# Trunk of attention and experts on one core: the residual sum in natural column order, normalised in place, a weight place freed for the stream, and the last expert columns in halves

## The chip, the core and the metric

The kernel runs on one core of a Trainium2 chip. The metric is device time in microseconds, the median of the runs shown; lower is better. Rows of the profile give times from the start of the span. TensorE (PE), VectorE (DVE), ScalarE (ACT), GpSimd (POOL) and SyncE (SP) are the engines; SyncE issues all DMAs here.

## What is computed

256 tokens of width 2048 pass through one layer: three attention branches, gates and an output projection w_o, a residual sum with a layer norm, then a mixture of 32 experts (each token goes to two experts of one group of eight), and a second residual sum with a layer norm:

```python
merged = g_a * (o_a @ w_up_a[l]) + g_b * (o_b @ w_up_b[l]) + g_c * (o_c @ w_up_c[l])
x = layer_norm(ALPHA * x + merged @ w_o[l], ln1_g[l], ln1_b[l])
y = hier_moe(x, w_grp[l], b_grp[l], w_rt[l], b_rt[l], w1[l], w3[l], w2[l])
x = layer_norm(ALPHA * x + y, ln2_g[l], ln2_b[l])
...
for e in range(N_EXPERTS):
    hid = jax.nn.silu(xt @ w1[e]) * (xt @ w3[e])
    out = out + comb[:, e:e + 1] * (hid @ w2[e])
```

All is float32. The experts' weights w1, w3 and w2 are 3 x 32 matrices of 4 MB, read once, 403 MB of the 540 MB that the kernel reads.

## The kernel before, in words

**Up to w_o.** Every projection is cut into units (`proj`, L175): `ld` loads 256 KB of weights into one of six places of a ring in the tile `stt` (L164, L186), `sp` splits it into a high and a low part (a cast on ScalarE, L155, a subtraction on VectorE, L156), `run` makes the matmuls (L215 to L217 for w_o). `emit` (L609) writes them out so that loads run five units and splits two units ahead of the matmuls. A ring place is loaded again when the split of its last load is done; SyncE issues in order, so a load that waits holds back all that stand behind it. Within these limits a scheduler orders an engine's instructions; those in `V(...)` keep the order of the program among themselves.

**w_o (L508 to L511).** 64 units: two halves of the contraction, each over column blocks `WO` (L437) of 512, 512, 512, 256 and 256. After the first half of a block `residual_sum` (L468) adds ALPHA * x, which `load_x` (L439) has put into the tile `wx` after unit `XL` (L44), and after the second half it adds the rest; the two token chunks of 128 are c = 0 and 1. `wx` holds the sum as [t, j, p], with the column blocks of the contraction contiguous, so that `row_stats` (L475), the transposes of `logit_step` (L501) and its logit matmuls (L505) read contiguous columns. Between the units, after those of `WOL` (L43), one part of the experts' stream is issued (`main.load`, L819).

**The stream (`Stream`, L665).** The experts' weights are parts of 2 MB, in the order of use, each loaded by SyncE into a free place of 16 KB a partition. The first parts go in halves of 1 MB (`HALVES`, L40). Places: four (`wk`, `wkk`), four (`wg`), `acc` and `yb` once each, and `wx`, once both token chunks are normalised out of it (L926). A place is loaded again when `used` (L740) tells that its part, or half of it, is through. The parts 0 to 8 are loaded up to the end of w_o; part 9 goes into `yb` (L887), part 10 into `wx` (L927), parts 11 to 14 into the places of parts 0 to 3, in halves.

**Between w_o and the experts (L885 to L927).** Per token chunk: statistics, 1/sqrt on GpSimd, then `normalise` (L830) writes the normalised sum in another layout into memory of `stt` and a tile `x1n`, four pieces of 512 columns, half of them on ScalarE, half on GpSimd; `route_steps` (L845) finds group, experts and positions on VectorE with a few small matmuls (L875), and a selection matrix S (L881). `keep_warm` (L629) puts small bf16 matmuls into TensorE's gaps, `KW` of them (6 and 6). Then `gather` (L988) picks the rows of each expert by matmuls with S (weights are the normalised sum, 128 x 128, L991), and `hidden` (L1025) makes the products, four experts beside each other. The first call of it does four of eight steps and frees the first halves of its places (L1067).

**The experts.** 8 rounds of four experts: h1 and h3, their product, transposes (L1096, of every second column), w2 (L1113), `combine` (L1035). The first norm's residual is added in rounds 1 to 4 (`residual`, L966).

**The end.** In the last round w2 comes in slices of 1024, 512 and 512 columns (`LAST`, L663; L725), one DMA for each expert of the four in a 512-column slice. `last_slices` (L1122) makes the products in four steps (k, j), `combine` copies 512 columns, multiplies them by the weights of the routing for both token chunks and adds; `chain` (L1190) makes a chunk's statistics, and `fast_tail` (L1175) the second norm and the stores.

## Time and profile before

| | us |
|---|---|
| median of 3 runs | 1681.29 (1680.66 to 1682.52) |
| profiled execution, its own time | 1680.39 |
| its span, first to last instruction | 1678.6 |
| TensorE busy | 1458.4 (87%) |
| VectorE busy | 615.0 (37%) |
| ScalarE busy | 456.0 (27%) |
| GpSimd busy | 12.6 (1%) |
| mean DMA rate over the span | 324 GB/s |

The profiled execution is 1.79 us longer than its span. Busy shares are means over stages of different kinds; a stage is to be read by its own rows. A matmul of two float32 operands shows as two records, a transpose as one.

### The profile page before, as it was taken

What the parts mean: (1) busy time and instruction counts of PE and PEld (TensorE: products, weight loads), DVE (VectorE), ACT (ScalarE), POOL (GpSimd) and SP (SyncE); (2) the same over time, 40 slices, a digit from 0 to 9 for tenths busy, and PEclk for the clock granted to TensorE, in tenths of its full rate; (3) what the DMA queues carried; (4) which work ended last, traced back from release to release, by engine and by line L of the source; (5) the groups of instructions that cost most, each with busy time, mean ns of one, the idle gap of its engine ahead of it and who ended that gap; (6) DMA issues with size and microseconds to landing.
All of it is one profiled execution on the core that took longest, in us unless ns stands there. A gap on an engine that the chain in (4) does not pass through costs nothing.

```text
span 1678.6 us, 20715 instructions
## 1 busy us (share of the span) xinstructions
PE 1458.4 (87%) x7984; PEld 878.5 (52%) x7984; DVE 615.0 (37%) x1165; ACT 456.0 (27%) x841; POOL 12.6 (1%) x24
## 2 busy tenths in 40 slices
PE   9999999999999999998976967967868768769758
PEld 8989988888878887883321322312312212213212
DVE  6656866566565676551120210200200101101005
ACT  5545455665545444441100000000000000000100
POOL 0000000000000000010000000000000000000000
PEclk9999999999999999999987987978978879879879
DMA  7766565555887558959999999999999999999996
GB/s 238 230 188 169 157 171 163 175 170 177 279 299 230 185 183 276 329 187 380 429 426 429 428 427 429 428 426 428 427 428 428 428 428 428 427 429 428 428 413 230
DMA packets 120203, 543.67 MB, mean 324 GB/s; under 512 B 13904, under 2 KB 28064, under 8 KB 94880
## 3 DMA queue, kind: packets, MB, share of 16 engines
q1 hardware_dynamic: 120096, 542.27, 84.5%
q8 instruction: 64, 1.05, 0.3%
q14 instruction: 43, 0.35, 0.1%
HBM read 540.10 MB, written 2.12 MB: 323 GB/s over the span
## 4 chain that ended last, share of the span: by engine, by line
PE 54%; DMA 42%; DVE 1%; issue 1%; ACT 1%; SPq 1%; POOL 0%; ACTq 0%; DVEq 0%; POOLq 0%
DMA wg<-in_w_dram 15%; DMA wk<-in_w_dram 15%; PE ps L216 10%; PE ps L217 9%; PE ps L215 9%; PE h L1030 9%; DMA wkk<-in_w_dram 5%; DMA wx<-in_w_dram 4%; PE yp L1113 3%; PE ps L210 3%; PE ps L207 3%; PE ps L209 3%; DMA stt<-in_w_gate_dram 1%; PE yp L1136 1%; DMA stt<-in_w_o_dram 1%
## 5 line engine op out<-in xcount | busy, mean ns | idle before, releaser
L156 DVE TENSOR_TENSOR wl<-stt,wh 128x512 fp32r<-128x512 f32 (+1 forms) x492 | 333.7, 684 | 238.7 <-ACT wh L155 237.4
L155 ACT CAST wh<-stt 128x512 fp32r<-128x512 f32 (+1 forms) x492 | 302.1, 616 | 315.0 <-PE ps L217 129.8
L1030 PE MATMUL h<-wg,xg 128*32 128x512 f32 x896 | 230.2, 703 | 74.3 <-DMA wg<-in_w_dram 74.2
L1030 PE MATMUL h<-wk,xg 128*32 128x512 f32 x704 | 200.8, 709 | 58.0 <-DMA wk<-in_w_dram 58.0
L215 PE MATMUL ps<-wh,xH 128*128 128x512 f32 (+2 forms) x512 | 198.1, 389 | 0.3 <-ACT wh L155 0.2
L216 PE MATMUL ps<-wl,xH 128*128 128x512 f32 (+2 forms) x512 | 195.3, 381 | 2.9 <-DVE wl L156 2.8
L217 PE MATMUL ps<-wh,xL 128*128 128x512 f32 (+2 forms) x512 | 194.8, 381 | 0.0
L1001 DVE TENSOR_SCALAR xg<-gp,g1n,b1n 128x128 f32<-128x128 f32 x56 | 22.9, 410 | 424.9 <-PE h L1030 373.6
L1030 PEld LDWEIGHTS h<-wg,xg 128*32 128x32 f32 x896 | 50.7, 126 | 190.0 <-DMA wg<-in_w_dram 101.9
L1030 PE MATMUL h<-wkk,xg 128*32 128x512 f32 x208 | 117.0, 718 | 18.2 <-DMA wkk<-in_w_dram 18.2
L1030 PE MATMUL h<-wx,xg 128*32 128x512 f32 x208 | 114.2, 703 | 12.1 <-DMA wx<-in_w_dram 12.1
L998 ACT ACTIVATE xg<-gp,b1n,g1n 128x128 f32<-128x128 f32 x56 | 25.6, 457 | 356.5 <-PE h L1030 252.5
L1030 PEld LDWEIGHTS h<-wk,xg 128*32 128x32 f32 x704 | 44.0, 127 | 144.1 <-DMA wk<-in_w_dram 81.2
L216 PEld LDWEIGHTS ps<-wl,xH 128*128 128x128 f32 x512 | 96.7, 189 | 22.6 <-DVE wl L156 5.4
L215 PEld LDWEIGHTS ps<-wh,xH 128*128 128x128 f32 x512 | 96.3, 189 | 18.3 <-ACT wh L155 1.6
L217 PEld LDWEIGHTS ps<-wh,xL 128*128 128x128 f32 x512 | 96.6, 189 | 17.4
L1113 PE MATMUL yp<-wg,yb 128*32 128x512 f32 x368 | 95.0, 595 | 6.8 <-DMA wg<-in_w_dram 6.8
L1113 PE MATMUL yp<-wk,yb 128*32 128x512 f32 x304 | 91.4, 596 | 7.0 <-DMA wk<-in_w_dram 7.0
L1039 DVE COPY yb<-yp 128x512 f32<-128x512 f32 x15 | 10.4, 691 | 189.9 <-PE yp L1113 173.0
L207 PE MATMUL ps<-xH,wh 128*128 128x256 f32 x256 | 73.3, 286 | 0.0
L210 PE MATMUL ps<-xH,wl 128*128 128x256 f32 x256 | 72.7, 284 | 0.2 <-DVE wl L156 0.2
L209 PE MATMUL ps<-xL,wh 128*128 128x256 f32 x256 | 72.6, 284 | 0.0
(322 smaller groups left out, 1991.9 us busy)
## 6 DMA issues: line engine op xcount, KB each, us to landing
wg<-in_w_dram SPq DMA_DIRECT2D x75, 2048.0 KB, 27.6
wk<-in_w_dram SPq DMA_DIRECT2D x57, 2048.0 KB, 28.2
stt<-in_w_gate_dram SPq DMA_DIRECT2D x192, 256.0 KB, 3.1
wx<-in_w_dram SPq DMA_DIRECT2D x20, 2048.0 KB, 27.1
wkk<-in_w_dram SPq DMA_DIRECT2D x18, 2048.0 KB, 30.2
stt<-in_w_in_dram SPq DMA_DIRECT2D x104, 256.0 KB, 3.0
stt<-in_w_o_dram SPq DMA_DIRECT2D x64, 256.0 KB, 5.8
wg<-in_w_dram SPq DMA_DIRECT2D x14, 1024.0 KB, 8.5
```

The source lines that it names most:

```text
L155: nc.scalar.copy(h, src)
L156: nc.vector.tensor_tensor(l, src, h.bitcast(F32), ALU.subtract)
L207: nc.tensor.matmul(o, hb, a.H(kt), start=st_ and b % 2 == 0, stop=False, skip_group_check=True)
L209: nc.tensor.matmul(o, hb, a.L(kt), start=False, stop=False, skip_group_check=True)
L210: nc.tensor.matmul(o, lb, a.H(kt), start=False, stop=sp_, skip_group_check=True)
L215: nc.tensor.matmul(o, ha, wh, start=st_, stop=False)
L216: nc.tensor.matmul(o, ha, wl, start=False, stop=False)
L217: nc.tensor.matmul(o, la, wh, start=False, stop=sp_)
L998: nc.scalar.activation(xg[:, kt], gp[:, j], AF.Identity, scale=g1n[:, kt:kt + 1], bias=b1n[:, kt:kt + 1])
L1001: nc.vector.tensor_scalar(xg[:, kt], gp[:, j], g1n[:, kt:kt + 1], b1n[:, kt:kt + 1], ALU.mult, ALU.add)
L1030: nc.tensor.matmul(h[32 * e:32 * e + 32, :], xg[:, 8 * c + j, 32 * e:32 * e + 32], wt[e][:, j, :], start=(c == 0 and j == 0), stop=(c == 1 ...
L1113: nc.tensor.matmul(yps[n][32 * e:32 * e + 32, :], hT[:, 2 * k + j, 32 * e:32 * e + 32], wt[e][:, j, n * 512:(n + 1) * 512], start=(k + j = ...
```

## The change

The sum is kept in natural column order: `x1p` is [t, 2048]; x is loaded into places of the staging ring, at later units (`XL`), and read from there with a stride; the transposes take every nj-th column (4th or 2nd). `normalise` works in place, on ScalarE alone, by 512 columns, and `gather` reads every 8th column. The tiles `stt` and the split weights' buffers are closed after w_o and their memory becomes `wq`, a place of the stream, loaded right behind `yb`; `wx` is no place any more. `keep_warm` is called six times, with one tile. Parts 11 to 14 go in a quarter, a quarter and a half, and the first product frees its places by quarters after two steps. In the last round a slice of 512 columns comes in two DMAs, one for the even and one for the odd rows of all four experts; the last step of the last slice and `combine_last` work in halves of 256 columns, the copy on ScalarE and VectorE; statistics of the second norm are over 256 columns.

```diff
-XL = (1, 5, 12, 18, 22)
-KW = (6, 6)
+XL = (3, 11, 19, 23, 27)
+KW = (6, 6, 6, 10, 4, 12)
...
-    wb = ctx.enter_context(tc.tile_pool(name="wb", bufs=1))
-    stt = wb.tile([P, 6 * 512], F32, name="stt")
...
-    wsp = ph1.enter_context(tc.tile_pool(name="wsp", bufs=3, side="right"))
+    wss = ExitStack()
+    wb = wss.enter_context(tc.tile_pool(name="wb", bufs=1, side="right"))
+    stt = wb.tile([P, 6 * 512], F32, name="stt")
+    wsp = wss.enter_context(tc.tile_pool(name="wsp", bufs=3, side="right"))
...
-            nc.sync.dma_start(x1p[c][:, kt:kt + w // P], xp[c * P:(c + 1) * P, kt:kt + w // P, :])
+            XR[i, c] = st = stg()[:, :w].rearrange("t (j p) -> t j p", p=P)
+            nc.sync.dma_start(st, xp[c * P:(c + 1) * P, kt:kt + w // P, :])
+    def cols_of(i, c):
+        o, w, _ = WO[i]
+        return x1p[c][:, o:o + w]
...
-        a = x1p[c][:, kt:kt + nj]
-        return nc.vector.scalar_tensor_tensor(a, a, 1.0 if half else ALPHA,
-                                              ps[:, :w].rearrange("t (p j) -> t j p", j=nj), ALU.mult, ALU.add)
-    def row_stats(c, k):
-        return nc.vector.bn_stats(R["st"][:, c, k // 2, :], x1p[c][:, k:k + 2].rearrange("t j p -> t (j p)"))
+        a = cols_of(i, c)
+        if half:
+            return nc.vector.scalar_tensor_tensor(a, a, 1.0, ps[:, :w], ALU.mult, ALU.add)
+        return nc.vector.scalar_tensor_tensor(a.rearrange("t (p j) -> t p j", j=nj),
+                                              XR.pop((i, c)).rearrange("t j p -> t p j"), ALPHA,
+                                              ps[:, :w].rearrange("t (p j) -> t p j", j=nj), ALU.mult, ALU.add)
+    def row_stats(i, c, k):
...
-            nc.tensor.transpose(tp[:, j, :], x1p[c][:, kt + j, :], ident)
+            nc.tensor.transpose(tp[:, j, :], cols_of(i, c)[:, j::nj], ident)
         xt = R["xs"] if nj == 4 else R["xs"][:, 2 * c:2 * c + 2]
-        R["xc"] = nc.scalar.copy(xt[:, :nj], tp[:, :nj])
+        V(nc.scalar.copy(xt[:, :nj], tp[:, :nj]))
+        if between:
+            between()
...
-                self.jobs = [(k, h) for k in u[:a] for h in range(2)] + [(k, None) for k in u[a:b]]
-                self.jobs += [(k, h) for h in range(2) for k in u[b:c]] + [(k, None) for k in u[c:]]
+                self.jobs = [(k, h) for k in u[:a] for h in ((0, 2), (2, 4))] + [(k, (0, 4)) for k in u[a:b]]
+                self.jobs += [(k, h) for h in ((0, 1), (1, 2), (2, 4)) for k in u[b:c]] + [(k, (0, 4)) for k in u[c:]]
...
+                if ne == 4:
+                    for j in range(2):
+                        nc.sync.dma_start(t.rearrange("p (x j n) -> p x j n", j=2, n=w)[:, :, j],
+                                          w2[4 * q:4 * q + 4, c * 256:(c + 1) * 256,
+                                             o:o + w].rearrange("x (p j) n -> p x j n", j=2)[:, :, j])
+                    return
...
+    wss.close()
+    wqp = ctx.enter_context(tc.tile_pool(name="wqp", bufs=1, reuse_waits="tile"))
+    wq = wqp.tile([P, W2D], F32, name="wq")
     main.add([yb2], True)
+    main.add([wq])
...
+    def normalise(c, *ks):
+        for k in ks:
+            v = x1p[c][:, 512 * k:512 * k + 512]
+            V(nc.scalar.activation(v, v, AF.Identity, scale=rs1[:, c:c + 1], bias=nb1[:, c:c + 1]))
...
+        normalise(c, *(range(4) if c else range(2)))
...
+    main.load()
...
-    keep_warm(KW[0])
-    logit_step(len(WO) - 1, 1)
+    warm = keep_warm(KW[0])
+    logit_step(len(WO) - 1, 1, lambda: keep_warm(KW[1], warm))
+    normalise(0, 2, 3)
+    keep_warm(KW[2], warm)
     for k in "ababab":
...
-    keep_warm(KW[1])
+    keep_warm(KW[3], warm)
     for k in "caca":
         next(steps[k])
-    main.add([wx])
-    main.load()
 
...
-                pin(nc.tensor.matmul(gp[:, j, :], x1n[c][k4 // 2][:, 4 * (k4 % 2) + j, :], S[:, c].rearrange("p e s -> p (e s)"),
+                pin(nc.tensor.matmul(gp[:, j, :], x1p[c][:, k4 // 2 * 1024 + k4 % 2 * 4 + j:(k4 // 2 + 1) * 1024:8], S[:, c].rearrange("p e s -> p (e s)"),
...
+            keep_warm(KW[4], warm)
             for _ in steps["c"]:
                 pass
+            keep_warm(KW[5], warm)
...
-                hidden(0, 0, "1", xg, h1, 0, 4)
+                hidden(0, 0, "1", xg, h1, 0, 2)
+                hidden(0, 0, "1", xg, h1, 2, 4)
...
+        def combine_last(o, yp, then=None):
+            cut = [slice(256 * h, 256 * h + 256) for h in range(2)]
+            y = yb[:, o:o + 512]
+            V2(nc.scalar.copy(y[:, cut[0]], yp[:, cut[0]]))
+            V2(nc.vector.tensor_copy(y[:, cut[1]], yp[:, cut[1]]))
+            for c in range(2):
+                cp = PS["pm"].tile([P, 512], F32, name=f"cp{q}{o}{c}", tag="lg" if c else "lt")
+                for h in cut:
+                    nc.tensor.matmul(cp[:, h], ScT[:, c, :], y[:, h], start=True, stop=True, skip_group_check=True)
+                for k, h in enumerate(cut):
+                    a = acc[c][:, o:o + 512][:, h]
+                    V2(nc.vector.tensor_tensor(a, a, cp[:, h], ALU.add))
+                    if then:
+                        then(c, k)
...
+                        cut = (0, 256, 512) if end and k + j == 2 else (0, 512)
...
+                            for a, b in zip(cut, cut[1:]):
+                                for e in range(4):
+                                    nc.tensor.matmul(yp[32 * e:32 * e + 32, a:b], hT[:, 2 * k + j, 32 * e:32 * e + 32],
+                                                     wt["n", q, k, (n, e // ne)][:, e % ne, j, i * 512 + a:i * 512 + b],
+                                                     start=(k + j == 0), stop=(k + j == 2), skip_group_check=True)
                 for i, yp in enumerate(yps):
```

## Rows read from the trace of the kernel before

**Rows 1.** The page's slices: the span in 40 equal parts of 42 us; the granted TensorE clock in tenths of full speed, and what the DMA moved.
```profile
PEclk9999999999999999999987987978978879879879
GB/s 238 230 188 169 157 171 163 175 170 177 279 299 230 185 183 276 329 187 380 429 426 429 428 427 429 428 426 428 427 428 428 428 428 428 427 429 428 428 413 230
```

**Rows 2.** Busy time by stretches: from:to in us, its length, then busy us (records) of PE, of PE's weight loads, DVE, ACT and POOL, the granted clock (1.00 is 2.4 GHz), the DMA share and GB/s.
```profile
660.00:670.00 10.00, 9.76 (x42) 7.55 (x41) 6.33 (x10) 5.31 (x9) 0.00 (x0) 1.00 1.04 403
735.00:747.00 12.00, 11.89 (x99) 11.29 (x98) 5.19 (x15) 4.20 (x8) 1.16 (x2) 1.00 0.01 2
760.00:762.20 2.20, 2.20 (x25) 0.47 (x17) 0.05 (x1) 0.46 (x1) 0.00 (x0) 1.00 0.02 7
764.50:1603.00 838.50, 647.24 (x3490) 211.83 (x3486) 106.46 (x182) 48.20 (x97) 0.00 (x0) 0.87 1.01 428
1632.00:1655.00 23.00, 19.24 (x106) 5.44 (x110) 5.76 (x10) 0.59 (x1) 0.00 (x0) 0.85 1.02 364
```

**Rows 3.** Timeline of SyncE around the end of w_o: start, us, the DMA issues of the stream's parts by the place that they fill.
```profile
746.97 0.34 SPq L733 DMA_DIRECT2D yb<-in_w_dram  x1
752.60 0.34 SPq L733 DMA_DIRECT2D wx<-in_w_dram  x1
762.24 1.28 SPq L733 DMA_DIRECT2D wk<-in_w_dram  x3
766.90 1.28 SPq L733 DMA_DIRECT2D wk<-in_w_dram  x3
```

**Rows 4.** w_o's loads. First the line of its DMA issues from 630 to 746 us, from issue to landing; then the waits of ScalarE in w_o (us in total, times, longest); then four rows of the timeline: two casts one unit apart, and the two places at 660 us where TensorE waits for late weights.
```profile
DMA to landing us min/median/max: 2.9/5.5/8.3
...
ACT wh L155 <- DMA stt<-in_w_o_dram: 15.4, 9, 2.8
...
725.68 0.62 ACT L155 CAST wh<-stt 128x512 fp32r<-128x512 f32 x1 [0.74 <-DVE wl L156]
...
727.04 0.62 ACT L155 CAST wh<-stt 128x512 fp32r<-128x512 f32 x1 [0.74 <-DVE wl L156]
...
660.60 0.19 PEld L215 LDWEIGHTS ps<-wh,mH 128*128 128x128 f32 x1 [0.45 <-ACT wh L155]
...
661.33 0.50 PE L216 MATMUL ps<-wl,mH 128*128 128x512 f32 x1 [0.22 <-DVE wl L156]
```

**Rows 5.** Transposes on TensorE. The weight loads of the two lines, with ns min/median/max, first and last start, and one burst of each from the timeline: L501 reads contiguous columns, L1096 every second one.
```profile
L501 PEld LDWEIGHTS xt<-ident,wx x32: 138/140/144, 704.4 to 747.7; 128*128 128x128 f32 x32
...
L1096 PEld LDWEIGHTS ht<-ident,yb x32: 194/209/218, 800.4 to 1629.2; 128*128 128x128 f32 x32
...
718.54 1.03 PE L501 MATMUL xt<-ident,wx 128*128 128x128 f32 x8
...
800.42 0.71 PE L1096 MATMUL ht<-ident,yb 128*128 128x128 f32 x4 [0.93 <-DVE yb L1091]
```

**Rows 6.** Routing and first gather: rows of the timeline (start, us, records), then the stretch in which the clock is low (columns as in rows 2), a later burst of the same gather, and the piece of the chain of waits that is the first half of the first product.
```profile
750.10 0.85 ACT L841 ACTIVATE stt<-wx,nb,rs 128x512 f32<-128x512 f32 x1 [1.56 <-DVE nb L848]
...
750.17 0.80 POOL L843 TENSOR_SCALAR stt<-wx,rs,nb 128x512 f32<-128x512 f32 x1 [0.70 <-DVE nb L848]
...
750.38 0.72 DVE L881 TENSOR_TENSOR S<-posm,io 128x128 f32<-128x128 f32 x1
...
751.21 3.75 PE L991 MATMUL g<-S,stt 128*128 128x128 f32 x16 [0.47 <-DVE S L881]
...
754.94 3.72 PE L991 MATMUL g<-S,stt 128*128 128x128 f32 x24
755.11 0.19 DVE L879 SCALAR_TENSOR_TENSOR posm<-pos,o 128x32 f32<-128x32 f32 x1 [1.50 <-PE cnt L948]
...
755.33 0.29 DVE L881 TENSOR_TENSOR S<-posm,io 128x128 f32<-128x128 f32 x1
...
749.90:756.40 6.50, 6.04 (x37) 5.82 (x38) 4.64 (x27) 3.14 (x4) 2.40 (x3) 0.50 0.98 381
...
814.31 1.06 PE L991 MATMUL gp<-S,stt 128*128 128x128 f32 x8
...
758.66 3.57 PE h L1030 x32
```

**Rows 7.** The tail. First the last part's DMA (L726, its one issue at 1649.2, from issue to landing), then the timeline from the last products to the last copy, then VectorE's groups of 256 columns in w_o (count, busy us, mean ns): the sum and the statistics.
```profile
L726 SPq DMA_DIRECT2D wk<-in_w_dram x1: 827/827/827, 1649.2 to 1649.2; - x1
...
DMA to landing us min/median/max: 11.1/11.1/11.1
...
1658.33 3.83 PE L1136 MATMUL yp<-wk,yb 128*32 128x512 f32 x30
...
1662.19 0.58 ACT L1041 COPY yb<-yp 128x512 f32<-128x512 f32 x1 [5.83 <-PE yp L1136]
...
1664.00 0.69 DVE L1048 TENSOR_TENSOR acc<-acc,cp 128x512 f32<-128x512 f32 x1 [3.09 <-PE cp L1044]
...
1667.19 1.41 DVE L1228 SCALAR_TENSOR_TENSOR acc<-acc,mv,wg 128x512 f32<-128x512 f32 x2
...
1673.76 0.58 ACT L1243 COPY acc<-w 128x512 f32<-128x512 f32 x1 [4.59 <-PE w L1221]
...
L476 DVE BATCH_NORM_STATS2 st<-wx 128x6 f32<-128x256 f32 x15 | 5.4, 413 | 0.0
...
L472 DVE SCALAR_TENSOR_TENSOR wx<-wx,ps 128x256 f32<-128x256 f32 x7 | 2.7, 416 | 2.9 <-PE ps L217 2.9
```

More of the change, by code (lines that the diff above doesn't have):

```diff
@@ L459, in ev @@
             for c in cs:
-                for k in range(kt, kt + nj, 2):
-                    row_stats(c, k)
+                for k in range(0, nj, 2):
+                    row_stats(i, c, k // 2)
             for c in cs:
@@ L715, in load_now @@
             assert self.ready()
-            k, half = self.jobs[self.i]
+            k, part = self.jobs[self.i]
             self.i += 1
@@ L731, in load_now, with used @@
             src = w[4 * q + e, c * r:(c + 1) * r, :].rearrange("(p j) n -> p (j n)", p=P)
-            sl = slice(0, W2D) if half is None else slice(half * D, (half + 1) * D)
+            sl = slice(*(x * W2D // 4 for x in part))
             nc.sync.dma_start(t[:, sl], src[:, sl])
         def need(self, key):
-            while key not in self.slot or any(j[0] == key for j in self.jobs[self.i:self.i + 8]):
+            while key not in self.slot or any(j[0] == key for j in self.jobs[self.i:self.i + 12]):
                 self.load()
             return self.slot[key][0]
-        def used(self, keys, h=1):
+        def used(self, keys, n=4):
             for k in keys:
@@ L745, in used @@
                     self.free.append((t, k))
-                self.done |= {(k, 0), (k, h)}
+                self.done |= {(k, i) for i in range(n)}
             while self.i < len(self.jobs) and self.ready():
@@ L979, in stats2 @@
     def stats2(c, o, w):
[L980 to L981 removed]
+        for k in range(o // 256, (o + w) // 256):
+            nc.vector.bn_stats(st2[:, c, k, :], acc[c][:, k * 256:(k + 1) * 256])
     def moe_round(ws, first):
@@ L1032, in hidden, with combine @@
                                      skip_group_check=True)
-            ws.used(keys, int(j1 == 8))
-        def combine(q, o, w, yp, ScT, then=None):
+            ws.used(keys, j1 // 2)
+        def combine(q, o, w, yp, ScT):
             sln = slice(o, o + w)
             y = yb[:, sln]
-            if (o // 512) % 2 and then is None:
+            if (o // 512) % 2:
                 nc.vector.tensor_copy(y, yp[:, :w])
@@ L1188, in prefill, with chain @@
             V2(nc.tensor.matmul(t, ident, b2[:, i * 512:(i + 1) * 512], start=True, stop=False))
-        def chain(c):
-            V2(nc.vector.bn_stats(st2[:, c, 3, :], piece(c, 3)))
+        def chain(c, half):
+            V2(nc.vector.bn_stats(st2[:, c, 6 + half, :], piece(c, 3)[:, 256 * half:256 * half + 256]))
+            if half == 0:
+                return
             V2(nc.vector.bn_aggr(mv2[:, c], st2[:, c]))
@@ L1255, in hybrid_trunk @@
             more = Stream(False)
-            more.add([t for t in slots if t is not main.ln] + [wx])
+            more.add([t for t in slots if t is not main.ln] + [wq])
             moe_round(more, False)
```

55 lines of the change are left out of this document (17 added, 38 removed).

## The prediction, made before the changed kernel ran

> **What bounds the kernel now.** I read the page's slices first. In the first 17 slices (of 42 us) the DMA moves 157 to 329 GB/s and the granted clock is at 9 tenths or more; from the 20th slice on it moves 426 to 429 GB/s, the last two apart [rows 1]. The stretches say it with borders: from 764.5 to 1603 us the DMA share is 1.01 at 428 GB/s, while TensorE is busy for 647 of 838 us [rows 2]. So the experts' stage is a stream of 2 MB weight parts at the DMA's own pace. In front of it lies a stretch in which all places of the stream are full: from 735 to 747 us the DMA moves 2 GB/s, TensorE is busy for 11.89 of 12 us [rows 2]. SyncE then issues one part at 746.97 (its memory comes free when w_o's last matmul is through), one at 752.60, and at 762.24 the first that goes into a place which the experts have used [rows 3]; between, from 760 to 762.2 us, the DMA is idle again [rows 2]. From 762.24 on nothing but bytes counts. Therefore a change is worth three things: how much earlier that first reuse comes, whether the stream keeps its rate, and how long the tail is behind the last landing.
>
> The first reuse has its own chain: w_o's matmuls end, the routing follows, the gather, then the first half of the first product (758.66 for 3.57 us) [rows 6]. The tail: the last part is issued at 1649.2, lands 11.1 us later (1660.3), and the kernel ends 18.3 us after that [rows 7].
>
> **The change part by part**, against the profiled execution's own time, 1680.39 us (span 1678.6 and 1.79 around it); the median of the runs, 1681.29, lies 0.90 higher.
>
> *The extra place.* wq is loaded behind yb at once, instead of the 752.60 issue. That part then lands some 4 us earlier, but nothing waits for it before the first reuse: both kernels have eleven parts on the chip by then. Worth 0 alone; it closes the idle 760 us stretch only if the reuse comes earlier. The number of bytes left is the same.
>
> *First reuse by quarters.* The half of the first product that frees them now (32 records, two for a float32 matmul, 3.57 us [rows 6]) is cut at two of its four steps, so the first places come free 1.8 us earlier. Four DMAs of 0.5 MB are issued then and four more 1.8 us later, 4 MB or 10 us of stream, so the queue doesn't run dry before the next halves (4.66 us apart now [rows 3]). SyncE issues twelve pieces there instead of eight, 0.43 us each (1.28 for three [rows 3]), while the stream is ahead of it, and eight fewer at the end: 0. What the smaller pieces cost isn't in the trace; the bounds are nothing and the rate of the narrow slices at the end, 364 against 428 GB/s [rows 2], on 4 MB: 1.7 us. Their rows are 4 KB, twice the narrow slices' rows, so I take 0.4. Net -1.4.
>
> *Normalising.* Four GpSimd pieces leave, ScalarE does eight of 512. A ScalarE piece costs 0.85 us in the layout of now, at 750.10 for the second token chunk [rows 6]; that chunk's first two are done by 751.8 and needed at about 753.7: covered; without that cover they would cost up to 1.7 us. The first chunk's two stay on ScalarE where its two are now. VectorE loses a competitor: the same comparison takes 0.72 us while GpSimd works and 0.29 without [rows 6], so the first token chunk's selection is 0.4 us earlier, and, an estimate from the same row, the second's routing up to 1 us earlier, as it meets the same pieces.
>
> *The clock of the gather.* Behind w_o, TensorE has little to do, and from 749.9 to 756.4 us its granted clock is 0.50, the lower level (1.2 GHz) [rows 6]. So 16 gather records take 3.75 us, and 24 more 3.72 partly at that level; the same matmuls go at 0.11 us each later (8 in 1.06) [rows 6]. The routing of the second chunk waits 1.50 us for TensorE in the middle of it [rows 6]. The change puts 44 small matmuls into that gap instead of 12. If the clock holds: selection ready 750.45, 16 records at 0.145 (below) to 752.8, the second chunk's position matmuls and selection 0.9 us to 753.7, 16 records to 756.1; with some of the 8 others that were slipped in before it, the first product starts at 756.6 instead of 758.66. Added matmuls of 0.055 to 0.11 us lie in idle time; up to 0.5 us of them may stand in the way, which takes -2.0 as the sum. Bounds: 0 (the clock falls as now) and -2.8.
>
> *Strided weights.* The residual sum lies in natural column order now, so transposes read every 4th or 2nd element, and the gather every 8th. The trace has one strided weight load, the transposes of hb (every 2nd): 209 ns a load against 140, and spaced 0.143 us ((0.71-0.28)/3) against 0.109 [rows 5]. I take that row, +0.034 each: 32 transposes in w_o, where TensorE has no idle time, +1.1; the 32 gather records are counted above. Bounds: 0, and a doubled 0.109 us. [...]
>
> *x through the staging ring.* Ten loads of x leave wx, take ring places, and hold them until the residual sum reads them. A w_o unit is 1.36 us [rows 4]. The loads behind them are issued two units later than now (four units ahead, 5.4 us, not 8.2), and the two that reuse an x place wait for the residual sum on SyncE, with all later loads and stream parts queued behind: due 5 units after it, less cast and subtraction (1.3) and the sum itself (0.7), 4.8 us. Landings are 2.9 to 8.3 us, median 5.5, and the DMA is full there (1.04) [rows 4, 2]. So stalls up to 3.5 us at each of five places are possible. For it: now four x loads come at the head of the stage, and the two late weights that they cause cost TensorE 0.45 and 0.22 us and more [rows 4]; spread out, that goes, and the landings shorten with the backlog. Bounds -0.7 and +8. I take 0, as the backlog that makes 8 us landings is mostly these early issues themselves.
>
> *VectorE in w_o:* sums and statistics keep their shapes; a strided read is hidden beside TensorE. Later gathers are slower by a few us per group of experts, hidden in the idle quarter of TensorE's time.
>
> *Tail.* Now the last 512 columns start at 1658.33 and end 3.83 us later, 1.9 us behind the landing [rows 7]; with all experts' even rows in one DMA and odd rows in the last, 8 of 32 records are left at the landing, 0.95 us, and the first half of columns is through 0.45 us before. Copy in halves on two engines, then two halves of matmul: the first sum comes at about 1662.2 instead of 1664.00 [rows 7]. VectorE then has eight ops of 0.41 instead of four of 0.69 (+0.5) and eight groups to aggregate instead of four (0.1 a chunk, an estimate): 3.9 us against 3.2, so its next step starts at 1666.1 instead of 1667.19, and its ten remaining ops end 1.1 us earlier [rows 7]. The ScalarE copy at 1673.76 [rows 7], last now, comes earlier by more, as the first chunk's statistics are done 2 us earlier. Stores follow as now: -1.4 (bounds -0.5 and -2.2).
>
> **Sum:** -1.4 -2.0 +1.1 +0 -1.4 = -3.7: 1676.7 for a profiled execution, 1677.6 as the median, 0.22% less. About 0.2% (3.4 us) is what a measurement of this kernel can tell from no change.
>
> **Rivals.** (1) *The clock falls again:* the small matmuls are short, and idle gaps remain between them. For it: only the routing's own chain keeps TensorE waiting, and that stays. Then 2.0 are lost: 1679.6. (2) *Strided loads at double spacing:* w_o +2.9 in place of 1.1, and 32 gather records +0.11 each eat the 2 us: 1681.3. Against it: the one strided row. (3) *The ring starves w_o (slower):* VectorE reads x late, SyncE holds the next w_o load back, and TensorE, busy without a break now, waits. It decides when a landing there takes more than 4.8 us; at 6.4 us, between the median and the longest of now, five places cost 1.6 each, 8 us: 1685.6. (4) The stream hides it all: not possible here, as the DMA is idle in front of the first reuse and full behind it.
>
> **How the numbers follow.** Forecast 0.46, with a range of its own from 1673.5 to 1677.9; rival 1 0.17, rival 2 0.20 (both within 0.2%), rival 3 0.17. Faster by over 0.2%: 0.46, within 0.2%: 0.37, slower: 0.17. The low end takes the good bounds (0, -0.7, -2.8, -1.8, -2.2, 7.5 in all): 1673.5. The high end takes in rivals 1 and 2 and the milder part of 3: 1683.5.
>
> **What would show it.** Right: w_o's last matmul near 748 us; granted clock 1.00 from there on; the first reuse issued near 759.5 (762.24, +1.1, -2.0, -1.8); no GpSimd piece; transposes spaced near 0.14 us; the last landing near 1658; the end 17 us behind it. Wrong: matmuls of w_o waiting for casts behind an x load; the clock at 0.50 before the gather; the stream below 428 GB/s after 765 us; or narrow slices by rows that land at another rate than 364 GB/s.

## The result, and the profile after

The changed kernel is slower: 1692.31 us median (4 runs, 1690.91 to 1694.48) against 1681.12 for the kernel before on the same chip (4 runs, 1680.66 to 1682.52), ratio 1.0069, 95% interval 1.0056 to 1.0081. The forecast was 1677.6 with a range to 1683.5, so sign and range were both wrong. The profiled execution of after took 1692.95 us, span 1691.2: 12.6 us more than the span of before. Five borders, read in both traces, share them out:

| border, us from the start | before | after | difference |
|---|---|---|---|
| w_o's last matmul ends | 746.94 | 755.70 | +8.76 |
| first product starts, behind that | 11.65 | 13.08 | +1.43 |
| first reuse issued, behind that | 3.65 | 1.94 | -1.71 |
| last part lands, behind that | 897.97 | 899.62 | +1.65 |
| end of the span, behind that | 18.40 | 20.82 | +2.42 |

The first product is counted from its first record here. The page's slices look as in [rows 1]: from the 20th slice on the stream again moves 426 to 429 GB/s, the last two apart.

```profile
GB/s 238 230 188 163 162 169 161 176 173 177 303 293 213 185 179 258 294 190 373 428 429 427 428 427 428 427 427 428 427 428 428 427 427 427 426 428 429 428 408 199
```

Stretches of after, with the columns of [rows 2]. From 680 to 700 us, in w_o, TensorE lacks 2.5 of 20 us while the DMA is not full (0.83); the granted clock of 0.91 there is a stretch of 3.4 us at 0.50 (from 689.4 us), behind TensorE's longest wait for a late cast, 2.5 us up to 687.4. From 764 to 770.7 the DMA falls idle again ahead of the first reuse. The experts' stream has the 428 GB/s of before; the stretch of narrow slices has 337. The last line goes from the landing of the last wide part to the last landing, in which 8 MB of narrow slices land; the same stretch of before stands below it.

```profile
680.00:700.00 20.00, 17.47 (x116) 16.33 (x115) 10.78 (x17) 6.41 (x11) 0.00 (x0) 0.91 0.83 269
740.00:752.00 12.00, 11.96 (x98) 11.53 (x98) 6.06 (x13) 4.72 (x9) 0.00 (x0) 1.00 0.06 19
764.00:770.70 6.70, 6.70 (x41) 5.34 (x44) 2.72 (x13) 1.69 (x4) 0.00 (x0) 1.00 0.51 214
774.00:1613.00 839.00, 686.19 (x3519) 268.26 (x3522) 103.96 (x183) 48.63 (x98) 0.00 (x0) 0.88 1.01 428
1642.00:1668.00 26.00, 23.47 (x129) 6.72 (x133) 10.14 (x21) 1.17 (x2) 0.00 (x0) 0.87 0.96 337
1647.13:1670.34 23.21, 21.24 (x133) 5.67 (x132) 11.49 (x24) 1.17 (x2) 0.00 (x0) 0.97 0.87 298
```
```profile
1638.77:1660.21 21.44, 20.70 (x129) 5.60 (x130) 10.51 (x17) 1.17 (x2) 0.00 (x0) 0.96 0.89 316
```

SyncE's issues around the end of w_o, against [rows 3]: both free places are filled at once, and the first reuse comes at 770.72.

```profile
755.73 0.34 SPq L756 DMA_DIRECT2D yb<-in_w_dram  x1
756.31 0.34 SPq L756 DMA_DIRECT2D wq<-in_w_dram  x1
...
770.72 1.28 SPq L756 DMA_DIRECT2D wk<-in_w_dram  x3
```

w_o's loads against [rows 4]: the line of issues, their landings, and waits from 640 to 756 us (in total, times, longest). A median landing of 4.9 us instead of 5.5, and yet ScalarE's casts wait longer, 4.7 us at worst instead of 2.8, and TensorE behind them. Of the ten waits of the casts, 21.1 us, four are for loads that took 7.0 to 7.9 us to land (12.7 us) and four for loads that landed in under 4 us and had been issued late (5.8 us). SyncE stands for places that x holds (`DVE wx`, the last two lines).

```profile
L187 SPq DMA_DIRECT2D stt<-in_w_o_dram x64: 327/328/1572, 634.7 to 738.5; - x64
...
DMA to landing us min/median/max: 2.8/4.9/7.9
```
```profile
ACT wh L156 <- DMA stt<-in_w_o_dram: 21.1, 10, 4.7
...
PEld ps L216 <- ACT wh L156: 6.5, 5, 2.5
PE ps L216 <- ACT wh L156: 4.4, 3, 2.3
```
```profile
SPq L446 <- DVE wx L482: 5.1, 4, 2.0
SPq L187 <- DVE wx L482: 3.8, 5, 1.4
```

Transposes and gather, against [rows 5, 6]: the lines of the two weight loads, then the routing's timeline, the stretch of the gather and the chain. The strided transposes load in 212 ns, as the row of hb let expect; the gather's loads take 336 ns (192 with neighbouring columns, below). 16 of its records take 4.07 us although the clock is at 1.00, longer than the 3.75 us that they took before at 0.50. The traces give the clock as a share of full speed, and no run shows it in GHz; at the two levels `keep_warm`'s matmuls stand 0.056 us (1.00) and 0.107 us (0.50) apart.

```profile
L512 PEld LDWEIGHTS xt<-ident,wx x32: 195/212/218, 713.3 to 756.4; 128*128 128x128 f32 x32
```
```profile
L1004 PEld LDWEIGHTS g<-S,wx x64: 312/336/338, 759.3 to 782.1; 128*128 128x128 f32 x64
```
```profile
757.22 4.34 ACT L859 ACTIVATE wx<-wx,nb,rs 128x512 f32<-128x512 f32 x6
...
758.91 0.29 DVE L896 TENSOR_TENSOR S<-posm,io 128x128 f32<-128x128 f32 x1
...
759.25 4.07 PE L1004 MATMUL g<-S,wx 128*128 128x128 f32 x16
...
763.38 5.48 PE L1004 MATMUL g<-S,wx 128*128 128x128 f32 x22
```
```profile
760.00:766.00 6.00, 6.00 (x32) 5.99 (x33) 2.11 (x14) 3.11 (x5) 0.00 (x0) 1.00 0.99 419
```
```profile
768.86 3.57 PE h L1043 x32
```

The tail against [rows 7]: the last DMA in the chain (1654.72 + 15.62 = 1670.34), the timeline, and the stretch of the combining matmuls. The last products end 1.1 us behind the landing instead of 1.9, as planned. But the copy on VectorE starts only when the one on ScalarE is through, the first sum comes 4.2 us behind the landing (3.8 before), and the clock is at 0.57.

```profile
1654.72 15.62 DMA wk<-in_w_dram
```
```profile
1670.39 1.07 PE L1169 MATMUL yp<-wk,yb 128*32 128x256 f32 x16 [1.31 <-DMA wk<-in_w_dram]
1671.55 0.37 ACT L1146 COPY yb<-yp 128x256 f32<-128x256 f32 x1 [7.22 <-PE yp L1169]
1671.95 0.42 DVE L1147 COPY yb<-yp 128x256 f32<-128x256 f32 x1 [2.60 <-ACT yb L1146]
...
1671.97 3.38 PE L1151 MATMUL cp<-yb,xs 128*128 128x256 f32 x8 [0.52 <-ACT yb L1146]
1674.54 0.42 DVE L1154 TENSOR_TENSOR acc<-acc,cp 128x256 f32<-128x256 f32 x1 [2.16 <-PE cp L1151]
...
1679.00 1.40 DVE L1264 SCALAR_TENSOR_TENSOR acc<-acc,mv,wg 128x512 f32<-128x512 f32 x2
```
```profile
1672.00:1676.00 4.00, 4.00 (x10) 2.92 (x11) 1.77 (x5) 0.00 (x0) 0.00 (x0) 0.57 0.00 0
```

### The profile page after: what moved, and what is told of

It is laid out like the page before. It is cut to its first block, busy times and chain, and to the rows that moved or that the text cites. A ratio compares the mean times of both kernels' runs of the same rounds, so it can differ in the third digit from the quotient of the medians.

```text
span 1691.2 us, 20819 instructions
## 1 busy us (share of the span) xinstructions
PE 1503.2 (89%) x8028; PEld 941.0 (56%) x8028; DVE 614.9 (36%) x1176; ACT 458.4 (27%) x845; POOL 8.4 (0%) x18
## 4 chain that ended last, share of the span: by engine, by line
PE 54%; DMA 41%; DVE 2%; issue 1%; SPq 1%; ACT 1%; POOL 0%; DVEq 0%; ACTq 0%; POOLq 0%
DMA wk<-in_w_dram 15%; DMA wg<-in_w_dram 15%; PE ps L217 9%; PE ps L218 9%; PE ps L216 9%; PE h L1043 8%; PE yp L1127 4%; DMA wq<-in_w_dram 4%; DMA wkk<-in_w_dram 4%; PE ps L211 3%; PE ps L208 3%; PE ps L210 3%; DMA stt<-in_w_o_dram 2%; PE g L1004 1%; DMA stt<-in_w_gate_dram 1%
## 5 line engine op out<-in xcount | busy, mean ns | idle before, releaser
L1014 DVE TENSOR_SCALAR xg<-gp,g1n,b1n 128x128 f32<-128x128 f32 x56 | 22.9, 410 | 457.6 <-PE h L1043 373.6
L1043 PE MATMUL h<-wq,xg 128*32 128x512 f32 x208 | 115.3, 709 | 9.0 <-DMA wq<-in_w_dram 9.0
L1004 PE MATMUL gp<-S,wx 128*128 128x128 f32 x448 | 114.5, 416 | 9.0 <-DVE yb L1111 4.7
L1004 PEld LDWEIGHTS gp<-S,wx 128*128 128x128 f32 x448 | 109.0, 335 | 23.3 <-issue 8.4
L217 PEld LDWEIGHTS ps<-wl,xH 128*128 128x128 f32 x512 | 96.6, 189 | 21.1 <-DVE wl L157 4.2
L1127 PE MATMUL yp<-wg,yb 128*32 128x512 f32 x368 | 90.7, 601 | 2.6 <-DMA wg<-in_w_dram 2.6
L1127 PE MATMUL yp<-wk,yb 128*32 128x512 f32 x304 | 86.5, 599 | 3.5 <-DMA wk<-in_w_dram 3.5
L216 PE MATMUL ps<-wh,mH 128*128 128x512 f32 (+1 forms) x192 | 69.8, 367 | 4.6 <-ACT wh L156 4.4
```

Of the source, the lines that this page charges most:

```text
L216: nc.tensor.matmul(o, ha, wh, start=st_, stop=False)
L217: nc.tensor.matmul(o, ha, wl, start=False, stop=False)
L1004: pin(nc.tensor.matmul(gp[:, j, :], x1p[c][:, k4 // 2 * 1024 + k4 % 2 * 4 + j:(k4 // 2 + 1) * 1024:8], S[:, c].rearrange("p e s -> p (e s) ...
L1043: nc.tensor.matmul(h[32 * e:32 * e + 32, :], xg[:, 8 * c + j, 32 * e:32 * e + 32], wt[e][:, j, :], start=(c == 0 and j == 0), stop=(c == 1 ...
L1127: nc.tensor.matmul(yps[n][32 * e:32 * e + 32, :], hT[:, 2 * k + j, 32 * e:32 * e + 32], wt[e][:, j, n * 512:(n + 1) * 512], start=(k + j = ...
```

## The experiments

Each was compared with the kernel before on its own chip. "w_o" below is the time from the issue of its first load to the end of its last matmul: 112.15 us in before, 121.04 in after. Profiled stretches come from one execution each; where a stretch is the same work in several kernels, its spread is given.

### w_o: the ring, the strides, or the sums

**x_direct** (after, x not through the ring):

```diff
-XL = (3, 11, 19, 23, 27)
+XL = (1, 5, 12, 18, 22)
-            XR[i, c] = st = stg()[:, :w].rearrange("t (j p) -> t j p", p=P)
-            nc.sync.dma_start(st, xp[c * P:(c + 1) * P, kt:kt + w // P, :])
+            nc.sync.dma_start(x1p[c][:, o:o + w], xp[c * P:(c + 1) * P, o:o + w])
```

> The kernel after, but x is laid out in natural column order and loaded straight into its place in wx, at the units of before (1, 5, 12, 18, 22); the first residual sum works in place on contiguous columns. Transposes and gather keep their strides. Theory A (x's loads in the ring hold back the weight loads of w_o): w_o's last matmul ends near 748 us instead of 755.73, the ScalarE casts stop waiting longer than 3 us for a load, the total falls by about 8 us to 1684. Rival B (the strided transposes of w_o cost it): w_o ends at 755 as in after, total 1692. Rival C (VectorE's first sum, 1.08 us instead of 0.68, makes the weight split late): also near 748 here; before_ring tells C from A.

1684.34 us, ratio 1.0026 (1.0015 to 1.0038); w_o 113.54, ends at 747.2. Some 60% of the loss is gone. A holds, but for a longest wait of 3.3 us where it had 3; B falls.

```profile
ACT wh L156 <- DMA stt<-in_w_o_dram: 15.6, 8, 3.3
PEld ps L216 <- ACT wh L156: 1.3, 2, 1.0
PE ps L216 <- ACT wh L156: 0.5, 1, 0.5
```

**before_ring** (before, x through the ring, nothing else):

```diff
-            nc.sync.dma_start(x1p[c][:, kt:kt + w // P], xp[c * P:(c + 1) * P, kt:kt + w // P, :])
+            XR[i, c] = st = stg()[:, :w].rearrange("t (j p) -> t j p", p=P)
+            nc.sync.dma_start(st, xp[c * P:(c + 1) * P, kt:kt + w // P, :])
```

> The kernel before with one part of the change alone: x through the six-place staging ring, at the units of after (3, 11, 19, 23, 27); layout, sums (contiguous reads of x, about 0.68 us), transposes, routing and tail as before. Theory A (ring places): w_o ends 6 to 9 us later than 746.97, total 1687 to 1690. Rival B (strided transposes): no change, 1681. Rival C (VectorE's strided sum): no change, 1681.

1688.78 us, ratio 1.0061 (1.0044 to 1.0078); w_o 119.06. The ring does it without any stride, and with the granted clock at 1.00 all through w_o; A holds, B and C fall.

```profile
ACT wh L155 <- DMA stt<-in_w_o_dram: 27.8, 15, 3.3
PEld ps L215 <- ACT wh L155: 5.8, 6, 2.1
PE ps L215 <- ACT wh L155: 3.8, 4, 1.6
```

**before_skip** and **before_late** ask which part of the ring: the first passes over ten places, the second only moves the x loads.

```diff
 # before_late
-XL = (1, 5, 12, 18, 22)
+XL = (3, 11, 19, 23, 27)
 # before_skip: the same, and behind each direct load of x
+            stg()
```

> The kernel before, x loaded straight into its place at the units of after (3, 11, 19, 23, 27), and at each of these units two places of the six-place ring are passed over unused. So the loads of w_o behind them wait for a place two units longer, as with x in the ring, but no place is held until VectorE has read x. before_ring took 119.06 us from the first load of w_o to its last matmul, before 112.15. Theory L (what costs is that SyncE stands at a place that x holds until the residual sum): 112 to 114 us here. Rival M (a load issued two units later is late whatever follows): 117 to 119.

> The kernel before with one number list changed: x is loaded straight into its place, but at the units of after (3, 11, 19, 23, 27). before_skip differs from it only by the ten places passed over. Theory M (the places are the cost): w_o from first load to last matmul 111.5 to 113 us, total as before. Rival Y (the later x loads, due soon after, push the weights aside): 116 to 119 us, total 5 to 6 us over before.

before_skip: 1686.12 us, ratio 1.0032 (1.0021 to 1.0042), w_o 118.55. L falls: no place is held by x there, and 7.7 of the 8.2 us between before_ring (119.06) and before_late (110.88) are lost all the same. The 0.5 us left for places that x holds is less than the same stretch differs between kernels (118.7 to 122.2 us in seven with the ring and the strides). before_late: 1678.57 us, ratio 0.9990 (0.9981 to 1.0000), w_o 110.88, a little under M's 111.5 to 113; its x loads alone do no harm. So the price lies in the two places at each of five units: a load issued two units (2.7 us) later. The waits of the two for loads:

```profile
ACT wh L155 <- DMA stt<-in_w_o_dram: 22.3, 10, 4.2
PEld ps L215 <- ACT wh L155: 6.2, 6, 1.9
PE ps L215 <- ACT wh L155: 4.3, 5, 1.4
```
```profile
ACT wh L155 <- DMA stt<-in_w_o_dram: 13.9, 9, 2.4
```

**x_direct_tplain** (x_direct, transposes on neighbouring columns, the router's weights laid out to match):

```diff
-            nc.tensor.transpose(tp[:, j, :], cols_of(i, c)[:, j::nj], ident)
+            nc.tensor.transpose(tp[:, j, :], cols_of(i, c)[:, j * P:(j + 1) * P], ident)
```

> The kernel x_direct, and the transposes for the router read 128 neighbouring columns of the sum instead of every 4th or 2nd (the router's weights laid out to match). From the first load of w_o to its last matmul x_direct takes 113.54 us, before 112.15. Theory N (the stride of 64 transposed records is the rest): 112.1 to 112.3, total 1.3 us under x_direct. Rival O (the rest is x's natural order or the sums): 113.5.

w_o 111.82, 1.7 us less; but six kernels with direct x and such transposes spread from 111.5 to 112.9, so the stride's part is 0.6 to 2.0. In the total nothing is to be seen (1684.30 us, 1.0021, 1.0011 to 1.0032): N for w_o, unresolved for the time.

### The gather: its stride and its clock

**gather_plain**, **gather_two** and **gather_four** replace the gather's every 8th column of the sum by neighbouring, every 2nd and every 4th ones. They leave out that the columns have to meet the experts' rows in the same order; the work is the same. gather_two and gather_four were executed once.

```diff
-x1p[c][:, k4 // 2 * 1024 + k4 % 2 * 4 + j:(k4 // 2 + 1) * 1024:8]
+x1p[c][:, k4 * 512 + j * P:k4 * 512 + (j + 1) * P]   # gather_plain
+x1p[c][:, k4 * 512 + j:(k4 + 1) * 512:4]             # gather_four
```

> The kernel after, but the gather's weights are 128 neighbouring columns of the normalised sum instead of every 8th (which columns meet which expert row is so changed; counts and order of all work stay). Theory D (the stride of the gather's weight loads doubles its records, 0.25 us each instead of 0.11): the 38 records ahead of the first product take 4.2 us instead of 9.6, the first product starts 4 to 5 us earlier after the end of w_o (13.05 us now), total 1687.5. Rival E (the gather waits for the routing, not for its own weights): no more than 1 us earlier, total 1691 to 1692.

> The kernel after, but the gather's weights are every 2nd column of the sum (which columns meet which expert row is so changed). A weight load took 192 ns on neighbouring columns, 329 on every 4th, 336 on every 8th. [...] Rival X (any stride costs a float32 load the same): 310 to 336 ns, 12.9 to 13.1 us.

> The kernel after, but the gather's weights are every 4th column of the sum instead of every 8th (which columns meet which expert row is so changed). Neighbouring columns gave 0.11 us a record and a first product 8.36 us behind w_o, every 8th column 0.25 and 13.08. Theory Q (what the transposes show at every 2nd and 4th column, a load 70 ns longer and 0.034 us more a record, holds for the gather too, and only 32 bytes is worse): 0.145 us a record, 9.6 us. Rival R (the gather's loads pay the whole at any stride): 0.25, 13.1.

First product behind the end of w_o: 8.36 us with neighbouring columns, 8.56 with every 2nd, 12.91 with every 4th, 13.08 with every 8th. In the traces the gain lasts to the last landing: w_o's end to there takes 910.0 and 910.9 us with neighbouring and every 2nd, 914.1 and 914.6 with every 4th and 8th. gather_plain's total, 1689.17, ratio 1.0066 (1.0049 to 1.0082), is not told apart from after's 1.0069, so the 4.7 us stand on the traces alone. D holds; E, Q and X fall. R's numbers came out at every 4th column, but its "any stride" falls with every 2nd. The weight loads of the three:

```profile
L1004 PEld LDWEIGHTS g<-S,wx x64: 186/192/192, 759.2 to 774.2; 128*128 128x128 f32 x64
```
```profile
L1004 PEld LDWEIGHTS g<-S,wx x64: 193/196/197, 756.6 to 771.8; 128*128 128x128 f32 x64
```
```profile
L1004 PEld LDWEIGHTS g<-S,wx x64: 307/329/330, 758.1 to 780.6; 128*128 128x128 f32 x64
```

**warm_less** (after with `KW = (6, 0, 0, 6, 0, 0)`):

> The kernel after with 12 of the small matmuls behind w_o instead of 44 (KW 6, 0, 0, 6, 0, 0). Theory J (they hold the granted clock at 1.00 through the gather): the clock falls to 0.50 from about 5 us behind w_o on, the gather gets slower and the first product starts 1 to 3 us later behind the end of w_o than 13.08. Rival K (the strided weight loads set the gather's pace at either clock, or the clock stays up): 13.1 as now, total 1692.

First product 13.42 us behind w_o, granted clock 0.83 from 755 to 765 (3.4 us of it at 0.50); 1692.12 us. J's clock falls, though for a shorter time than it had, and the price is K's: with strided loads the first product comes only 0.34 us later than in after (13.08).

### The tail

**tail_whole** (after, last 512 columns whole, `combine`, `chain` and `stats2` of before) and **tail_before** (the narrow slices by experts as well).

```diff
-                    V2(nc.scalar.copy(y[:, cut[0]], yp[:, cut[0]]))
-                    V2(nc.vector.tensor_copy(y[:, cut[1]], yp[:, cut[1]]))
...
+                    nc.scalar.copy(y, yp[:, :w])
```

> The kernel after, but the last 512 columns are multiplied, copied, combined and summed whole, as before; the narrow slices of w2 still come by rows. Last landing to the end of the span is 20.86 us in after. Theory F (the halves cost: the copy on VectorE follows the one on ScalarE, VectorE's eight shorter operations stand in a fixed order behind eight matmuls): 17.5 to 18.3 us, total 1689 to 1690. Rival G (TensorE's clock, 0.5 to 0.6 from 1672 to 1676 us, costs it, since TensorE waits for the last landing from 1669 us on): the clock falls here too and the stretch stays above 19 us, total 1691 to 1692.

> The kernel tail_whole, and the narrow slices of w2 come by experts again (0.5 MB each), as before; of the tail's part of the change nothing is left. From the first product's first matmul to the last landing both before and after take 901.4 to 901.6 us, though the quarters free the first places 1.7 us earlier. Theory H (the slices by rows cost on the stream what the quarters gave): that stretch is 899.6 to 899.9 us here, the last products end 1.95 us behind the landing instead of 1.11, total about 0.9 us under tail_whole. Rival I (the quarters bring nothing): still 901.5, total about 0.8 us above tail_whole.

tail_whole: 1690.53 us, landing to end 18.36 instead of 20.82. gather_plain and x_direct, which have the halves but in whose trace the clock stays at 1.00, take 19.85 and 19.84. So the halves cost 1.5 us (F, whose 17.5 to 18.3 was missed by a little) and the fallen clock 1.0 (G's cause, though against G it did not fall in tail_whole). From the first sum to VectorE's first norm operation the whole columns need 3.2 us, the halves 4.5 (two lines of each, tail_whole and gather_plain, then the clock of gather_plain in that stretch):

```profile
1672.75 0.69 DVE L1061 TENSOR_TENSOR acc<-acc,cp 128x512 f32<-128x512 f32 x1 [3.89 <-PE cp L1057]
...
1675.94 1.41 DVE L1244 SCALAR_TENSOR_TENSOR acc<-acc,mv,wg 128x512 f32<-128x512 f32 x2
```
```profile
1668.88 0.42 DVE L1154 TENSOR_TENSOR acc<-acc,cp 128x256 f32<-128x256 f32 x1 [1.20 <-PE cp L1151]
...
1673.34 0.74 DVE L1264 SCALAR_TENSOR_TENSOR acc<-acc,mv,wg 128x512 f32<-128x512 f32 x1
```
```profile
1667.28:1669.50 2.22, 2.22 (x9) 1.82 (x10) 0.99 (x3) 0.00 (x0) 0.00 (x0) 1.00 0.00 0
```

tail_before: 1691.92 us, ratio as tail_whole (1.0068 and 1.0066): the totals can't tell H from I, and in its trace the first product to the last landing takes 901.2 us, near the 901.5 of Rival I. But that stretch has two parts. Up to the last wide part the quarters' gain is kept: it lands 878.4 to 878.7 us behind the first product in after, tail_whole and tail_before, 880.2 in before. The 8 MB of narrow slices behind it take 21.4 us in before, 22.5 in tail_before, 22.9 in tail_whole, 23.2 in after. Over all traces with these landings, eight by experts take 21.4 to 22.5 us and nine by rows 22.6 to 23.7, so H's mechanism shows, at 1.2 us in the mean, though the total that it foresaw does not. In each trace by rows one landing comes 3.9 to 5.1 us behind the one before instead of 2.6, and one SyncE issue takes 7.6 us; by experts the largest such gap is 1.7 to 2.7 us instead of 1.3, and no issue there takes longer than 4.8. What makes that issue long is open.

### Versions that keep what pays

**mend_four**, **mend_rows** (narrow slices by rows) and **mend_cold** (12 small matmuls) take x direct, plain transposes and the tail of before, and let ScalarE normalise into wq in the gather's order:

```diff
-            v = x1p[c][:, 512 * k:512 * k + 512]
-            V(nc.scalar.activation(v, v, AF.Identity, scale=rs1[:, c:c + 1], bias=nb1[:, c:c + 1]))
+            v = x1p[c][:, 512 * k:512 * k + 512].rearrange("t (p j) -> t j p", j=8)
+            V(nc.scalar.activation(part_of(c, k), v, AF.Identity, scale=rs1[:, c:c + 1], bias=nb1[:, c:c + 1]))
```

> A version meant to keep what pays: x loaded straight into its place in natural order, transposes on neighbouring columns, ScalarE normalises from there into wq in the gather's order (so the gather's weights are neighbouring columns too, and wx goes to the stream as in before), quarters and the 44 small matmuls as in after, narrow slices and tail as in before. Added up from the runs: w_o from first load to last matmul 111.8 us (before 112.15); first product 8.4 to 9.0 us behind it (11.65); first reuse 1.9 behind that (3.65); the stream from there 898.0 to 899.3 (897.97); the end 18.4 to 19.1 behind the landing (18.40). Sum against before: -0.3 -2.9 -1.7 +0.7 +0.4 = -3.8 us, 0.23% faster. Rival P (the copy into another layout makes ScalarE late and the gather waits): first product at 10 or later, sum -2 or less.

> The kernel mend_four with the narrow slices of w2 by rows, as in after. The last products end 0.84 us earlier behind the landing. Theory H (the slices by rows take 1.4 to 1.8 us longer on the stream): 0.6 to 1 us over mend_four. Rival I: 0.8 us under it.

> The kernel mend_four with 12 of the 44 small matmuls (KW 6, 0, 0, 6, 0, 0). In warm_less the clock fell to 0.83 and cost 0.3 us, with the gather's records at 0.25 us. Theory J (the small matmuls were worth 2 us to a gather without strides): the clock falls to 0.50 and the first product starts 1.5 to 2.5 us later behind w_o than in mend_four. Rival K: within 0.5 us.

mend_four 1681.36 us, ratio 1.0005 (0.9996 to 1.0014); mend_rows 1680.93, 1.0004 (0.9993 to 1.0016); mend_cold 1683.01, 1.0011 (1.0001 to 1.0021). P's mechanism came true, its start nearly (9.70 us behind w_o, between the 8.4 to 9.0 added up and P's 10): ScalarE's strided pieces take 1.31 us (0.80 in after), it is busy without a break from 748 to 757, and the first product stands still for its activations. By rows or by experts shows no difference in the total: by rows the narrow slices take 23.2 us instead of 22.1, and the end comes 18.62 us behind the landing instead of 19.38. mend_cold's first product starts 10.67 us behind w_o instead of 9.70, so the 32 further matmuls are worth some 1.0 us here, from one execution each. First ScalarE's line and TensorE's wait in mend_four, then the stretch from 750 to 754 of mend_four and of mend_cold, with the clock at 1.00 and 0.64:

```profile
L854 ACT ACTIVATE wq<-wx,nb,rs x8: 1302/1312/1332, 745.4 to 754.1; 128x512 f32<-128x512 f32 x8
```
```profile
757.37 0.63 PE L1040 MATMUL h<-wk,xg 128*32 128x512 f32 x3 [1.29 <-ACT xg L1008]
```
```profile
750.00:754.00 4.00, 3.78 (x37) 3.58 (x37) 2.61 (x18) 4.00 (x4) 0.00 (x0) 1.00 0.54 223
```
```profile
750.00:754.00 4.00, 3.53 (x21) 3.28 (x21) 2.41 (x16) 4.00 (x4) 0.00 (x0) 0.64 0.86 364
```

**order_four**, **order_more** and **order_late** lay the columns of x and of w_o out in the gather's order beforehand, so that everything reads neighbouring columns and ScalarE can normalise in place; order_more cuts the load of the norm rows into five, order_late loads x at the units of after.

```diff
+    order = np.arange(D).reshape(2, P, 8).transpose(0, 2, 1).reshape(-1)
+        ("xp", a["x"][0][:, order]), ... ("w_o", a["w_o"][0][:, order]),
```

> The kernel after with x straight into its place and whole last columns, narrow slices by experts, and the columns of x and w_o laid out in the gather's order beforehand: sums, transposes and gather all read neighbouring columns, ScalarE normalises in place, wq goes to the stream at the end of w_o, quarters and small matmuls as in after. Added up from the runs: w_o from first load to last matmul 111.8 us (before 112.15), first product 8.4 us behind it (11.65), first reuse 10.3 (15.30), end of w_o to last landing 908.8 to 910.0 (913.27), end 19.1 behind the landing (18.40). Theory S (the gain that was forecast was real, and the ring and the stride took it): 3 to 4 us faster than before, 0.2%. Rival T (the DMA was idle for only some 2 us ahead of the first reuse, so an earlier reuse is worth no more): w_o to last landing 911 to 912, 1 us faster or the same.

> The kernel order_four with the 32 KB load of the norm rows cut into five, so that the program issues four DMAs more, at a place where SyncE has nothing else to do. In before the final waits of SyncE have three semaphores left when the last store lands, in after all eight (the queues are taken in turn), and the end is 1.09 against 1.82 us behind the last store's landing. Theory U (that order is the difference): 1.1 us behind that landing, 0.7 us under order_four. Rival V: 1.8 as in order_four.

> The kernel order_four with the x loads at the units of after (3, 11, 19, 23, 27), still straight into their place. before_late: w_o from first load to last matmul 110.88 us instead of 112.15. Theory Z (x's loads are better late, and what the ring lost was its places alone): 111 us here (order_four 112.64), 1 to 1.7 us under order_four, 0.2 to 0.25% under before. Rival: 112.6, as order_four.

order_four: 1678.15 us, 0.9985 (0.9976 to 0.9994), some 2.5 us and so between T's 1 and S's 3 to 4. First product 8.30 us behind w_o, first reuse 10.23 (15.30 before); w_o to last landing is S's 909.2 (order_late 910.3; 912.4 to 913.3 in the four kernels with the routing of before). order_late: w_o 110.85 as Z had it; **1677.28 us, ratio 0.9979 (0.9970 to 0.9988)**, the lowest ratio here, with an interval that overlaps order_four's. order_more: 1678.22, 0.9990 (0.9981 to 0.9999), the same as order_four; its final waits stand as in before, but of the 0.7 us only some 0.25 show: neither U nor V. order_late around the end of w_o: both places filled, and the DMA at 0.97 from 748 to 756 us, just ahead of the first reuse at 756.97.

```profile
746.78 0.34 SPq L746 DMA_DIRECT2D yb<-in_w_dram  x1
747.36 0.34 SPq L746 DMA_DIRECT2D wq<-in_w_dram  x1
...
756.97 1.28 SPq L746 DMA_DIRECT2D wk<-in_w_dram  x3
```
```profile
748.00:756.00 8.00, 7.93 (x91) 6.89 (x91) 6.49 (x41) 6.96 (x12) 0.55 (x1) 1.00 0.97 391
```

## Why the prediction was wrong

Along the borders above the prediction had +1.1 (w_o), -2.0 (first product), -1.8 (first reuse), +0.4 (stream) and -1.4 (end); the traces gave +8.8, +1.4, -1.7, +1.7 and +2.4.

- **x through the ring, taken at 0 (bounds -0.7 and +8): the step that failed.** Rival 3 came true, near its size: 8 us in w_o. The prediction had both numbers in hand, 5.4 us of lead and a median landing of 5.5 with a longest of 8.3 [rows 4], and let the landings shorten with the backlog. Its own limit for the places that x holds, 4.8 us, lay below that median. The landings did shorten, by 0.6 us in the median; the longest stayed at 7.9, and the casts' waits for loads that took 7.0 us and more are 12.7 of the 21.1 us. Rival 3's mechanism was half right: it put the loss on SyncE standing for the residual sum, and before_skip shows the lost lead alone to cost 7.7 us. That spreading x out helps was right too, but by itself: with x straight into its place w_o takes 110.9 us at the later units (before_late, order_late) and 111.5 to 112.9 at the earlier ones. The clock's fall in after's w_o is not what the loss rests on: before_ring and before_skip lose 6 to 7 us against before at 1.00, and gather_four takes 121.1 us for w_o at 1.00.
- **Strided weights, +1.1 in w_o and 0.145 us a gather record.** In w_o the size fits (0.6 to 2.0), and no run tells it closer. In the gather it does not: 0.25 us a record, 4.7 us to the first product. The error was to carry a row of transposes (209 against 140 ns at every 2nd element) to the loads of a float32 product, which behave otherwise: they take 192 ns on neighbouring columns, 196 at every 2nd element, 329 at every 4th, 336 at every 8th. So every 2nd element costs a gather's load 4 ns and every 4th 137, where a transpose's load pays 69 at every 2nd already; what makes them differ no run shows.
- **Clock of the gather, -2.0.** The mechanism was right: the granted clock stayed at 1.00 where it had been 0.50 [rows 6]. Without the stride the first product starts 8.36 us behind w_o instead of 11.65, 3.3 earlier, against the 3.1 that the prediction's terms give without their stride. How near that is owes something to luck: the four kernels with the routing of before start it at 11.65 and 11.35 us (before and before_ring, with 6.8 us at 0.50) and at 10.53 and 10.66 (before_late and before_skip, with 3.4 us at 0.50). mend_cold, with 3.4 us at 0.50, puts 1.0 us on the added matmuls. In after the stride ate all of the gain and 1.4 us more.
- **Quarters, -1.4.** Right: the first reuse comes 1.94 us behind the first product's start instead of 3.65, and of these 1.7 us, 1.5 to 1.8 are still there when the last wide part lands (after, tail_whole and tail_before against before).
- **Tail, -1.4; it was +2.4.** The last products did end 0.84 us earlier. The two copies did not run side by side: VectorE's waited for ScalarE's (both write parts of one tile; whether that is the reason was not tried with separate tiles). VectorE's steps up to the first norm operation were priced at 3.9 us and took 4.5; the aggregation of eight groups alone takes 0.37 us instead of 0.26 a chunk. Not foreseen were the clock (1.0 us) and the very end: the last store's landing is followed by 1.82 us instead of 1.09.
- **Narrow slices by rows,** not priced beyond their records: the stream's last 8 MB took 21.4 us before and 23.2 in after, against which the 0.84 stand; mend_rows beside mend_four shows nothing left over.
- **Normalising and the extra place:** covered, as said; in after no GpSimd piece of it is left. order_four and order_late have both, together with the quarters and the clock, and are faster than before; what each is worth alone no run shows.
- **Slips in its sums,** too small to matter: rival 2 has +2.9 for 32 transposes at 0.109, which are 3.5; the selection at 750.45 is 0.2 us earlier than its rows give (750.38 + 0.72 - 0.43); the good bounds lead to 1673.8, not 1673.5.

## What to carry to other kernels

Taking places from a prefetch ring is a cut in lead for every load behind them (two of six places at each of five units cost w_o 7.7 us here): compare the lead that is left with the longest landing as well as with the median. A price read from one kind of instruction need not hold for another (every 2nd element cost a transpose's load 69 ns and a gather's 4), so look for a row of the same operation at the same stride before a layout change gets one. When parts of a change pull both ways, undo each alone: here what was left without them was worth 0.15% (order_four), and a ring, a stride and a split tail hid it.

## What was not expected of the hardware

- A strided read cost ScalarE and, in one shape, VectorE as well: a 128x512 normalisation took 1.31 us at every 8th element (mend_four) and 0.80 in a row (after); a residual sum of 512 columns whose staged operand is read every 128th element took 1.08 us against 0.68, but one of 256 columns 0.43 against 0.41.
- In after's tail TensorE's clock fell to 0.57 (from 1672 to 1676 us) behind a wait of 1.31 us for the last landing. In gather_four it fell in the same way behind 1.50 us, but in gather_plain, with a wait of 1.40 us at the same place, it stayed at 1.00. Why is open.
- SyncE's last act is to wait for eight semaphores of DMAs, in the same order in the traces of before and after. In after the last store's is the first, and all eight waits, 0.06 us each, come behind its landing (0.48 us); in before four do (0.22). The rest of the 0.7 us is in front of and in a drain of GpSimd that follows, and was not settled.
